# First expert's low weight parts behind its index list, its rows turned in four banks, second token tables at a later expert, last logits by halves

## The chip, the cores and the metric

The kernel runs on one core of one Trainium2 chip. The metric is the device time of one execution in microseconds (us), lower is better. Engines are named as the profile names them: PE (TensorE matmul; PEld is its weight load), DVE (VectorE), ACT (ScalarE), POOL (GpSimd), SP (SyncE, which issues plain DMAs here). Each engine works through its own list of instructions in the order in which the program wrote them.

## The reference, cut to what matters

One transformer layer over 2048 tokens of width 1024. A mixer (windowed attention and a bidirectional mLSTM) makes `x`, and then an expert layer in which each of 16 experts takes the 256 tokens with the highest affinity to it:

```
aff = softmax(h @ w_router)                    # 2048 x 16
gate, idx = top_k(aff.T, 256)                  # per expert
xg = h[idx]                                    # 16 x 256 x 1024
g, u = xg @ w_gate, xg @ w_up                  # 1024 -> 512
y = (silu(g) * u) @ w_down * gate              # 512 -> 1024
x = x + g2 * scatter_add(y at idx)
```

## The kernel before, in words

The mixer runs over 16 token tiles of 128 rows; each finished tile is normalised (`finish`), its router logits are made (`logits`, L2131) and its affinities are put into a table `aff` (`affinity`). After the last tile the expert phase (`phase_moe`) begins.

**Routing** (`route`). The 256th highest affinity of every expert is found by a search of 15 rounds (`search`, `counts`): DVE counts for two candidates (L2292), ACT for the third (L2280), PE sums (L2304, L2307), DVE takes the next candidates (L2331). Then come prefix sums, the position of every chosen token (L2441) and its split into two hexadecimal digits (`pb`, `pa`, L2448 and L2451). `picks` and `lists` turn the digits into index lists: one-hot tables on DVE, 16 matmuls over the token tiles (L2579), a small product `lm` (L2583 or L2585), one more matmul with a spreading matrix (L2590), `lw` (L2593) and `idx` (L2598). There are three lists: expert 0 alone, then experts 1 to 7, then experts 8 to 15. The tables of the two large lists take 32 DVE operations each (L2559, L2562) and lie in two of the four `y` buffers.

**Experts.** For expert e, POOL gathers its 256 rows in two tiles of 128 (`gathers`, L2610), PE turns them (16 transposes, L2628, two PSUM banks named `t`), ACT scales (`xv`, L2652), DVE casts to the high part (`xg_hi`, L2656), and DVE or POOL makes the low part (`less`, L2457). All matmuls use a high and a low part of each operand, three products each. PE makes gate and up columns in four units of 48 matmuls (`gu`, L2684), then 48 matmuls with the down weights (`yp`, L2736). `glu` and `silu_mul` make the hidden rows between them (`sg`, `h_hi`, `h_lo`). DVE scales the result into `y` (L2750), and POOL scatters it with an add into `out_x` (L2756), two scatters per expert.

**Weights.** Each expert has six pieces of 1 MB, loaded by SP (L2474) into five buffers `ew_raw`, split by ACT into `ew_hi` (L2529) and by DVE or POOL into `ew_lo` (L2457). Expert 0's first four pieces are split by quarters during routing: the high quarters (`high`, L2498) and the low quarters (`low`, L2490) are put one by one into the search rounds by `counts`, and what is left is put after it by `rest`.

**What sets the order.** A planner (`Flow`) runs the program as tasks in Python: each task says which engine it wants next and a guessed cost; a task gets an engine when it is ready and has the lowest number among those waiting (`PRE` lists these numbers; `main`, the expert matmuls, has 13). `Tokens` stand for buffers: a task that has taken one keeps it until `give`. The order in which the planner hands out the engines is the order of each engine's list on the chip; nothing is reordered there.

Of the kernel before, what the change touches and what calls it, by code (L numbers as in the profile page):

```python
# [59 lines left out]
PRE = dict(fill=2, route=3, w=3, oh=2, ol=9, gv=6, x=5, main=13, ws=1, wl=12, xs=8, h=13, down=0, y=2)  # L60
# [296 lines left out]
class Kernel:  # L357
# [1752 lines left out]
    def logits(self, i, users):  # L2110
# [16 lines left out]
        yield tok["t"]  # L2127
        pr = self.buf(self.ps, "t", [128, 16])
        yield "P", 1.73
        for k in range(8):  # L2130
            nc.tensor.matmul(pr, lhsT=xt[:, k, :], rhs=self.wr[:, k, :], start=(k == 0), stop=(k == 7))  # L2131
# [4 lines left out]
        fl.give(tok["t"])  # L2136
# [106 lines left out]
    def phase_moe(self):  # L2243
        nc, tc, a, s = self.nc, self.tc, self.a, self.s
        with ExitStack() as st:
# [15 lines left out]
            self.got, self.list_ev, self.gv_ev = Event(), evs(NE), evs(NE)  # L2261
            self.x_ev = [evs(4) for _ in range(NE)]
# [7 lines left out]
    def counts(self, x, cand, need, col, after):  # L2270
# [15 lines left out]
        lows = self.lo_todo[:1] if self.round > 4 else []  # L2286
        del self.lo_todo[:len(lows)]
# [10 lines left out]
        for g in lows:  # L2298
            self.fl.spawn(g, PRE["fill"])
# [45 lines left out]
    def route(self):  # L2345
# [90 lines left out]
        for hf in range(2):  # L2436
            nc.tensor.transpose(pt[:, hf, :], sel[:, hf * 128:(hf + 1) * 128], self.ident)
        pos = T([128, 2, 16, 8], "pos", I32)
# [65 lines left out]
    def rest(self):  # L2504
        while self.hi_todo or self.lo_todo:
            if self.hi_todo:
                yield from self.hi_todo.pop(0)
            if self.lo_todo:
                yield from self.lo_todo.pop(0)
# [22 lines left out]
    def picks(self):  # L2532

        nc, fl, keep = self.nc, self.fl, self.keep
        yield self.routed
        self.rp.__exit__(None, None, None)
        self.pg = self.pool("pgather", 2)
        p16 = self.p16
        oh = [keep.tile([128, 16, 16], F16, name=f"oh0{i}") for i in range(2)]
        for i in range(2):  # L2540
            yield V(256)
            nc.vector.tensor_tensor(oh[i], p16[i][:, 0, :, 0:1].to_broadcast([128, 16, 16]),
# [4 lines left out]
        yield from self.lists(0, 1, *oh)  # L2547
        fl.fire(self.list_ev[0])
        tok = self.tok["y"]
        for q in range(2):  # L2550
            oh = []
            if q:
                yield self.x_ev[1][3]
            for i in range(2):
                yield tok
                oh.append(self.buf(self.pin, "y", [128, D]).bitcast(F16).rearrange("p (c k e) -> p c k e", c=16, k=16))
            for k in range(16):
                yield V2(128)
                nc.vector.tensor_scalar(oh[0][:, :, k, :], p16[0][:, q], float(k), None, op0=OP.is_equal)  # L2559
                fl.follow()  # L2560
                yield V(128)
                nc.vector.scalar_tensor_tensor(oh[1][:, :, k, :], p16[1][:, q], float(k + 1),  # L2562
                                               self.ids[:, :, None].to_broadcast([128, 16, 8]), op0=OP.is_equal, op1=OP.mult)
                fl.follow()
            if q:
                yield self.x_ev[2][3]
            yield from self.lists(8 * q, 8, *(o.rearrange("p c k e -> p c (k e)") for o in oh))
            for j in range(max(8 * q, 1), 8 * q + 8):
                fl.fire(self.list_ev[j])
            for i in range(2):  # L2570
                fl.give(tok)

    def lists(self, e, n, ob, oa):
        nc, pg, fl, tok = self.nc, self.pg, self.fl, self.tok
# [11 lines left out]
        fl.give(tok["t"])  # L2586
        yield tok["t"]
# [12 lines left out]
    def gathers(self):  # L2600
        nc, s, fl, tok = self.nc, self.s, self.fl, self.tok
        for e in range(NE):
# [17 lines left out]
            self.xt[e] = hi, lo  # L2620
            for k2 in range(4):
                yield tok["t"]
                pt = self.buf(self.ps, "t", [128, 2, 256])
                yield "P", 0.43
                for j in range(2):
                    for t in range(2):
                        k = 2 * k2 + j
                        nc.tensor.transpose(pt[:, j, t * 128:(t + 1) * 128], xgs[t][:, k * 128:(k + 1) * 128], self.ident)  # L2628
                fl.spawn(self.xsplit(e, k2, pt, hi, lo), PRE["xs"])
# [15 lines left out]
    def xsplit(self, e, k2, pt, hi, lo):  # L2645
# [3 lines left out]
        for j in range(2):  # L2649
            k = 2 * k2 + j  # L2650
            yield "A", 0.45
            nc.scalar.activation(xv[:, j, :], pt[:, j, :], AF.Identity, bias=self.sh2[:, k:k + 1], scale=self.sc2[:, k:k + 1])  # L2652
        fl.give(tok["t"])
        h = hi[:, 2 * k2:2 * k2 + 2, :]
        yield V2(512)
        nc.vector.tensor_copy(h, xv)  # L2656
        yield from self.less((XSUB0 if e == 0 else XSUB)[k2], 512, lo[:, 2 * k2:2 * k2 + 2, :], xv, f(h))
# [167 lines left out]
```

## Time and profile before

| | us |
|---|---|
| median of 3 runs (lowest, highest) | 2040.84 (2037.56, 2042.3) |
| the profiled execution's own time | 2042.06 |
| span of its instructions | 2040.3 |
| PE busy, share of the span | 1863.0, 91% |
| DVE busy | 1595.5, 78% |
| ACT busy | 1280.7, 63% |
| POOL busy | 839.1, 41% |

The mixer takes the first 1400 us. The profiled execution is 1.2 us above the median of the runs. The profile's chain of what ended last gives 56% of the span to PE and 24% to DVE.

### The profile page before, as it was taken

How to read it: one execution, taken by the hardware profiler on the slowest of the kernel's cores; microseconds unless marked ns; L12 is line 12 of the kernel's file. 1: busy time of each engine (PE TensorE's matmuls, PEld its weight loads, DVE VectorE, ACT ScalarE, POOL GpSimd, SP SyncE). 2: the span in 40 equal slices, each digit the busy share in tenths (PEclk: the TensorE clock that was granted, in tenths of full speed). 3: DMA queues.
4: the chain of work that ended last, by engine and by line, in shares of the span. 5: the costliest groups of instructions: out<-in, count | busy, mean ns of one | idle time of the engine just before them, and what ended most of it. 6: DMA issues, size and time to landing. Idle time of an engine off the chain costs nothing.

```text
span 2040.3 us, 37000 instructions
## 1 busy us (share of the span) xinstructions
PE 1863.0 (91%) x12921; PEld 1665.6 (82%) x12921; DVE 1595.5 (78%) x3486; ACT 1280.7 (63%) x3144; POOL 839.1 (41%) x820
## 2 busy tenths in 40 slices
PE   7799999999999999996989989994589999999997
PEld 2698998899889989985767767783589999999996
DVE  3799779998998699868999677756667878787772
ACT  4477777787787777775665578865344545454542
POOL 0324234333543243316777665510334535353432
PEclk9899999999999999996999989996699999999999
DMA  8343264345342333227777867646467878888772
GB/s 281 98 145 102 73 189 123 109 149 160 99 120 79 95 84 97 79 82 205 270 255 260 286 224 242 225 145 222 133 203 210 261 226 253 240 235 254 223 233 42
DMA packets 293499, 357.82 MB, mean 175 GB/s; under 512 B 27288, under 2 KB 225592, under 8 KB 292416
## 3 DMA queue, kind: packets, MB, share of 16 engines
q1 hardware_dynamic: 283072, 320.32, 49.9%
q0 software_dynamic: 9376, 34.08, 7.2%
q8 instruction: 102, 1.67, 0.3%
q10 hardware_dynamic: 864, 1.05, 0.1%
q14 instruction: 85, 0.70, 0.1%
HBM read 270.73 MB, written 84.54 MB: 174 GB/s over the span
## 4 chain that ended last, share of the span: by engine, by line
PE 56%; DVE 24%; ACT 8%; DMA 6%; issue 5%; SPq 1%; POOL 0%; POOLq 0%; DVEq 0%; ACTq 0%
PE gu L2684 17%; PE mm L758 9%; PE yp L2736 8%; PE po L2004 5%; DVE w_lo L741 3%; PE t L303 2%; DMA w_raw<-in_w_in 2%; PE s L258 2%; PE o L593 1%; PE t L2628 1%; PE h L1912 1%; PE o L332 1%; PE o L331 1%; PE mm L776 1%; DVE s L280 1%
## 5 line engine op out<-in xcount | busy, mean ns | idle before, releaser
L2529 ACT ACTIVATE ew_hi<-ew_raw 128x1024 fp32r<-128x1024 f32 x184 | 193.6, 1056 | 163.6 <-PE yp L2736 91.5
L2457 DVE TENSOR_TENSOR ew_lo<-ew_raw,ew_hi 128x1024 fp32r<-128x1024 f32 x152 | 215.6, 1428 | 42.0 <-ACT ew_hi L2529 21.4
L291 POOL TENSOR_SCALAR P<-P,am 128x640 f32<-128x640 f32 (+1 forms) x128 | 113.1, 885 | 257.7 <-DVE am L289 145.4
L741 DVE TENSOR_TENSOR w_lo<-w_raw,w_hi 128x256 fp32r<-128x256 f32 (+1 forms) x352 | 157.3, 471 | 30.2 <-ACT w_hi L735 28.1
L2756 POOL DMA_INDIRECT out_x<-y,idx x32 | 57.1, 1786 | 260.7 <-DVE y L2750 175.0
L2684 PE MATMUL gu<-xg_hi,ew_hi 128*128 128x256 f32 x1024 | 148.6, 283 | 0.6 <-DVE xg_hi L2656 0.6
L758 PE MATMUL mm<-w_hi,hx_hi 128*128 128x256 f32 (+1 forms) x944 | 142.5, 288 | 5.2 <-ACT hxr L933 2.2
L735 ACT ACTIVATE w_hi<-w_raw 128x256 fp32r<-128x256 f32 (+1 forms) x352 | 135.2, 410 | 18.9 <-DMA w_raw<-in_w_in 18.1
L758 PE MATMUL mm<-w_hi,hx_lo 128*128 128x256 f32 (+1 forms) x944 | 141.9, 288 | 0.0
L2684 PE MATMUL gu<-xg_lo,ew_hi 128*128 128x256 f32 x1024 | 141.7, 280 | 0.0
L758 PE MATMUL mm<-w_lo,hx_hi 128*128 128x256 f32 (+1 forms) x944 | 141.5, 286 | 0.0
L2684 PE MATMUL gu<-xg_hi,ew_lo 128*128 128x256 f32 x1024 | 141.2, 280 | 0.0
L758 PEld LDWEIGHTS mm<-w_hi,hx_hi 128*128 128x128 f32 x944 | 124.8, 190 | 9.4 <-issue 2.7
L2684 PEld LDWEIGHTS gu<-xg_hi,ew_hi 128*128 128x128 f32 x1024 | 131.2, 189 | 1.0 <-DVE xg_hi L2656 0.9
L2684 PEld LDWEIGHTS gu<-xg_lo,ew_hi 128*128 128x128 f32 x1024 | 129.2, 189 | 0.0
L2684 PEld LDWEIGHTS gu<-xg_hi,ew_lo 128*128 128x128 f32 x1024 | 128.8, 189 | 0.0
L758 PEld LDWEIGHTS mm<-w_hi,hx_lo 128*128 128x128 f32 x944 | 125.0, 191 | 3.3 <-issue 2.6
L758 PEld LDWEIGHTS mm<-w_lo,hx_hi 128*128 128x128 f32 x944 | 124.6, 189 | 1.8 <-issue 0.9
L314 DVE TENSOR_TENSOR pl<-t,ph 128x512 fp32r<-128x512 f32 x156 | 105.8, 684 | 24.4 <-ACT ph L312 23.1
L282 ACT ACTIVATE P<-s,am 128x640 f32<-128x640 f32 (+1 forms) x128 | 99.8, 780 | 31.1 <-DVE am L280 25.7
L2750 DVE SCALAR_TENSOR_TENSOR y<-yp,gv,g2b 128x512 f32<-128x512 f32 x64 | 48.1, 751 | 90.2 <-PE yp L2736 90.2
L280 DVE CUSTOM_DVE_ANT_0 s<-s,mrow,nsink 128x640 f32<-128x640 f32 (+1 forms) x120 | 105.3, 877 | 13.1 <-PE s L262 7.5
(482 smaller groups left out, 5616.4 us busy)
## 6 DMA issues: line engine op xcount, KB each, us to landing
w_raw<-in_w_in SPq DMA_DIRECT2D x176, 256.0 KB
ew_raw<-in_w_gate SPq DMA_DIRECT2D x32, 1024.0 KB
ew_raw<-in_w_up SPq DMA_DIRECT2D x32, 1024.0 KB
ew_raw<-in_w_down SPq DMA_DIRECT2D x32, 1024.0 KB
xt<-in_w_mod SPq DMA_DIRECT2D x64, 256.0 KB
out_x<-xl SPq DMA_DIRECT2D x32, 512.0 KB
s_vs<-vsl SPq DMA_DIRECT2D x16, 516.0 KB
vsl<-s_vs SPq DMA_DIRECT2D x16, 516.0 KB
```

The costliest lines, as they stand in the source:

```text
L280: nc.vector.tensor_tensor_reduce(x, x, mask, 1.0, k.nsink[:, h:h + 1], op0=OP.add, op1=OP.min, accum_out=m[:, 0:1])
L282: nc.scalar.activation(P[:, :n], sc, AF.Exp, bias=m[:, 0:1], scale=-1.0, accum_out=m[:, 1:2])
L291: nc.gpsimd.tensor_scalar(P[:, :n], P[:, :n], m[:, 4:5], 0.0, op0=OP.mult, op1=OP.add)
L314: nc.vector.tensor_sub(lo, pt, f(hi))
L735: nc.scalar.activation(hi, raw[:, k:k + 2, :n], AF.Copy)
L741: nc.vector.tensor_sub(lo, raw[:, k:k + 2, :n], f(hi))
L758: self.nc.tensor.matmul(ps[:, :2 * n].rearrange("p (a b) -> p a b", a=2), lhsT=hx[:, k, t * 128:(t + 1) * 128], rhs=w[:, sl:sl + 2, k, :n] ...
L2004: self.nc.tensor.matmul(po, lhsT=m[:, k, :], rhs=self.wo[k0 + k][wi][:, sl], start=(j == 0), stop=(j == 11))
L2457: (self.nc.vector if eng == "D" else self.nc.gpsimd).tensor_sub(out, x, y)
L2529: nc.scalar.activation(hi[:, sl], raw[:, sl], AF.Copy)
L2684: nc.tensor.matmul(po[:, ft, :], lhsT=w[:, k, ft * 128:(ft + 1) * 128], rhs=x[:, k, :], start=(j == 0), stop=(j == 23))
L2736: nc.tensor.matmul(po[hf], lhsT=hs[i][h][:, ft, t * 128:(t + 1) * 128], rhs=wd[i][w][:, ft, hf * 512:(hf + 1) * 512], start=(j[hf] == 0), ...
```

## The change

1. `logits`: for the last two tiles the eight logit matmuls accumulate in a bank of `h2` and are issued in two halves of four, each behind its own half of the transposes.
2. The low quarters of expert 0's weights leave `counts` and `rest`; a new task `lows` issues them once expert 0's index list is made (first eight with number 1, the others with number 9).
3. `route` splits the positions of expert 0 by themselves first (16 columns in place of 256), so `picks` can begin its list before the large split.
4. `gathers`: the transposes of expert 0 go into four banks (two `t`, two `yp`), first all of the first row tile, then all of the second; one of its four scalings goes from ACT to DVE; the first product of `expert` waits for the high parts alone (`xh_ev`).
5. The tables of the two large lists become tasks `group(0)` and `group(1)` with numbers 10 and 14: group 0 waits for expert 0's rows to be split, group 1 for those of expert 3, its list for those of expert 4, and the second matmul of that list for expert 5's first piece.

```diff
-PRE = dict(fill=2, route=3, ..., main=13, ...)
+PRE = dict(fill=1, wl0=9, g0=10, g1=14, route=3, ..., main=13, ...)
...
@@ logits
+        last = i >= 2 * NT - 2
+        if last:
+            yield tok["h2"]
+            pr = self.buf(self.ps, "h2", [128, 2, 512])[:, 0, 0:16]
...
+            if last:
+                yield "P", 0.87
+                for k in range(4 * j, 4 * j + 4):
+                    nc.tensor.matmul(pr, lhsT=xt[:, k, :], rhs=self.wr[:, k, :], start=(k == 0), stop=(k == 7))
...
@@ counts
-        lows = self.lo_todo[:1] if self.round > 4 else []
-        del self.lo_todo[:len(lows)]
...
-        for g in lows:
-            self.fl.spawn(g, PRE["fill"])
...
@@ route
+        pos = T([128, 2, 8], "pos0", I32)
+        nc.vector.tensor_scalar(pos, pt[:, :, 0:8], 15.0, None, op0=OP.add)
...
+        fl.fire(self.routed0)
...
@@ rest
+    def lows(self):
+        yield self.hi_ev
+        for k in range(8):
+            yield from self.lo_todo.pop(0)
+        if self.lo_todo:
+            self.fl.spawn(self.lows(), PRE["wl0"])
...
@@ picks
+        fl.spawn(self.lows(), PRE["fill"])
         for q in range(2):
...
+            fl.spawn(self.group(q), PRE[f"g{q}"])
+
+    def group(self, q):
+        nc, fl, tok, p16 = self.nc, self.fl, self.tok["y"], self.p16
+        yield self.x_ev[3 * q][3]
...
+        if q:
+            yield self.x_ev[4][3]
+        yield from self.lists(8 * q, 8, *(o.rearrange("p c k e -> p c (k e)") for o in oh), q and self.x_ev[5][0])
...
@@ lists
+        if late:
+            yield late
         yield tok["t"]
...
@@ gathers
+            tags, pts = ("t", "t", "yp", "yp"), []
...
+            for k2 in range(4 if e == 0 else 0):
+                yield tok[tags[k2]]
+                pts.append(self.buf(self.ps, tags[k2], [128, 2, 256]))
+                yield "P", 0.22
+                turn(k2, (0,))
...
@@ expert
-                            yield self.x_ev[e][2 * k4]
-                            yield self.x_ev[e][2 * k4 + 1]
+                            for ev in (self.x_ev if xi else self.xh_ev)[e][2 * k4:2 * k4 + 2]:
+                                yield ev
```

**How the lists of the engines move.** PE, between expert 7's down product and expert 8's first columns (`yp` down product, `gu` columns, `t<-cst,xg` transposes of gathered rows, `spread` the last matmul of an index list). Before:

```order
L2736 MATMUL yp<-ew_lo,h_hi 128x512
L2628 MATMUL t<-cst,xg 128x128 x8
L2684 MATMUL gu<-xg_hi,ew_hi 128x256 x4
L2684 MATMUL gu<-xg_lo,ew_hi 128x256 x8
L2684 MATMUL gu<-xg_hi,ew_lo 128x256 x8
```

After:

```order
L2786 MATMUL yp<-ew_lo,h_hi 128x512
L2619 LDWEIGHTS spread
L2619 MATMUL t<-lm_22473,spread 128x128
L2656 MATMUL t<-cst,xg 128x128 x16
L2734 MATMUL gu<-xg_hi,ew_hi 128x256 x8
L2734 MATMUL gu<-xg_lo,ew_hi 128x256 x8
L2734 MATMUL gu<-xg_hi,ew_lo 128x256 x8
```

The last matmul of the list of experts 8 to 15 now stands behind the whole down product of expert 7, and all 16 transposes of expert 8 stand behind it, ahead of its first columns. Before, this list was made during expert 1, and the transposes here were those of expert 9.

POOL at the same place (`out_x` the scatter of an expert, `xg` a gather). Before, from expert 7's two scatters on:

```order
L2756 DMA out_x<-y,idx 2048x1024 x2
L2610 DMA xg<-s_xn,idx 128x1040
L2457 TENSOR_TENSOR xg_lo<-xv,xg_hi 128x512
L2610 DMA xg<-s_xn,idx 128x1040
L2457 TENSOR_TENSOR ew_lo<-ew_raw,ew_hi 128x1024
```

After, from expert 6's two scatters on:

```order
L2806 DMA out_x<-y,idx 2048x1024 x2
L2476 TENSOR_TENSOR ew_lo<-ew_raw,ew_hi 128x1024 x2
L2806 DMA out_x<-y,idx 2048x1024 x2
L2639 DMA xg<-s_xn,idx 128x1040 x2
L2476 TENSOR_TENSOR ew_lo<-ew_raw,ew_hi 128x1024
L2639 DMA xg<-s_xn,idx 128x1040
```

Between the scatters of expert 6 and those of expert 7 there is no gather any more; both gathers of expert 8 stand behind expert 7's second scatter.

DVE from the end of the selection to expert 0's index list, in the program after (`oh` the one-hot tables of expert 0, `pb` and `pa` the digits of all tokens):

```order
L2454 CAST p_19453<-part_19457 128x16
L2563 TENSOR_TENSOR oh_19460<-p_19452,lc 128x256
L2563 TENSOR_TENSOR oh_19461<-p_19453,lc 128x256
L2567 TENSOR_TENSOR oh_19461<-oh_19461,lc 128x256
L2460 TENSOR_SCALAR pos<-t 128x128 x2
L2467 TENSOR_SCALAR part_19469<-pos 128x256
L2470 CAST pb<-part_19469 128x256
L2467 TENSOR_SCALAR part_19489<-pos 128x256
L2470 CAST pa<-part_19489 128x256
L2610 CAST lm_19486<-t 16x16
L2622 TENSOR_TENSOR lw_19495<-t,lc 128x16
L2627 TENSOR_REDUCE idx<-lw_19495 128x2
```

Before, the six wide operations on `pos`, `part`, `pb` and `pa` stood ahead of the tables `oh`, and `lm` stood directly behind them; now they stand between `oh` and `lm`. Behind `idx` 11 low quarters follow in a row, where the 32 table operations of the first large list stood.

## Rows read from the trace of the kernel before

**Rows 1.** Busy us and instructions per engine in three stretches; PEclk is the granted clock.
```profile
core 0: us, PE busy (x) PEld busy (x) DVE busy (x) ACT busy (x) POOL busy (x), PEclk, DMA share, GB/s
1400.04:1458.88 58.84, 12.60 (x105) 9.73 (x106) 45.48 (x214) 21.41 (x54) 6.77 (x7) 0.50 0.61 203
1458.88:1543.98 85.10, 79.37 (x569) 74.30 (x570) 54.58 (x89) 38.53 (x53) 30.51 (x19) 0.96 0.59 175
1543.98:1579.04 35.06, 35.06 (x258) 33.12 (x258) 26.73 (x25) 17.93 (x25) 16.17 (x10) 1.00 0.82 241
```

**Rows 2.** Timeline, two rounds without a low quarter: start us, us, engine, instruction.
```profile
1405.13 0.16 DVE L2331 SCALAR_TENSOR_TENSOR cand<-hits,base 128x3 f32<-128x3 f32 x1
...
1406.78 0.16 DVE L2331 SCALAR_TENSOR_TENSOR cand<-hits,base 128x3 f32<-128x3 f32 x1
```

**Rows 3.** Chain of work that ended last, routing and expert 3: start us, us, what.
```profile
1417.46 0.17 DVE cand L2331
...
1428.70 0.17 DVE cand L2331
...
1431.65 0.45 issue
...
1437.08 0.60 DVE ew_lo L2490
...
1438.86 0.50 DVE pos L2441 x2
...
1442.93 0.18 DVE idx L2598
...
1579.04 19.61 PE gu L2684 x168
```

**Rows 4.** Timeline, end of the mixer and start of expert 0.
```profile
1394.46 1.96 PE L2131 MATMUL t<-wr,hx2t 128*128 128x16 f32 x16 [0.50 <-DVE lg L2135]
...
1445.62 1.12 POOL L2610 DMA_INDIRECT xg<-s_xn,idx  x1 [0.30 <-issue]
...
1447.73 0.28 DVE L2562 SCALAR_TENSOR_TENSOR y<-pa,lc 128x128 f16<-128x128 f16 x1
...
1451.34 0.15 DVE L2641 COPY gv<-xg 128x1 f32<-128x1 f32 x1 [1.03 <-DMA xg<-s_xn,idx]
...
1452.76 1.97 PE L2628 MATMUL t<-cst,xg 128*128 128x128 f32 x8 [0.38 <-DVE lw L2593]
...
1458.88 0.80 PE L2684 MATMUL gu<-xg_hi,ew_hi 128*128 128x256 f32 x2 [0.65 <-DVE xg_hi L2656]
```

**Rows 5.** Timeline, experts 0 and 1, where the second large list is made.
```profile
1475.69 6.71 DVE L2559 TENSOR_SCALAR y<-pb 128x128 f16<-128x128 f16 x1
...
1477.56 4.77 POOL L2457 TENSOR_TENSOR ew_lo<-ew_raw,ew_hi 128x1024 fp32r<-128x1024 f32 x2
...
1492.34 0.56 PE L2736 MATMUL yp<-ew_hi,h_hi 128*128 128x512 f32 x1
...
1514.68 0.23 PE L2590 MATMUL t<-lm,spread 128*128 128x128 f16 x1 [2.85 <-DVE lm L2585]
```

**Rows 6.** Timeline, the boundary between two experts in the steady stretch.
```profile
1574.33 1.03 PE L2628 MATMUL t<-cst,xg 128*128 128x128 f32 x8
...
1577.11 2.06 POOL L2756 DMA_INDIRECT out_x<-y,idx  x1 [5.39 <-DVE ew_lo L2457]
1579.47 1.01 POOL L2610 DMA_INDIRECT xg<-s_xn,idx  x1 [0.30 <-issue]
...
1580.28 3.76 DVE L2457 TENSOR_TENSOR ew_lo<-ew_raw,ew_hi 128x1024 fp32r<-128x1024 f32 x2 [1.28 <-issue]
...
1581.98 1.78 POOL L2610 DMA_INDIRECT xg<-s_xn,idx  x1 [0.17 <-issue]
...
1598.21 0.69 DVE L2707 TENSOR_TENSOR sg<-sg,gu 128x512 f32<-128x512 f32 x1 [0.89 <-PE gu L2684]
```

**Rows 7.** The gather's line, all 32: time from issue to landing.
```profile
DMA to landing us min/median/max: 4.1/7.7/9.5
```

More of the change, by code (lines that the diff above doesn't have):

```diff
@@ L2125, in logits @@
             fl.give(tok["t"])
+            if last:
+                yield "P", 0.87
+                for k in range(4 * j, 4 * j + 4):
+                    nc.tensor.matmul(pr, lhsT=xt[:, k, :], rhs=self.wr[:, k, :], start=(k == 0), stop=(k == 7))
         self.release(users)
[L2127 to L2131, printed above, removed]
+        if not last:
+            yield tok["t"]
+            pr = self.buf(self.ps, "t", [128, 16])
+            yield "P", 1.73
+            for k in range(8):
+                nc.tensor.matmul(pr, lhsT=xt[:, k, :], rhs=self.wr[:, k, :], start=(k == 0), stop=(k == 7))
         fl.give(tok["hx2t"])
@@ L2437, in route @@
             nc.tensor.transpose(pt[:, hf, :], sel[:, hf * 128:(hf + 1) * 128], self.ident)
+        pos = T([128, 2, 8], "pos0", I32)
+        yield V(16)
+        nc.vector.tensor_scalar(pos, pt[:, :, 0:8], 15.0, None, op0=OP.add)
+        fl.follow()
+        self.p0 = [T([128, 16], f"p0{i}", F16) for i in range(2)]
+        for i, (op, n) in enumerate(((OP.bitwise_and, 15), (OP.logical_shift_right, 4))):
+            part = T([128, 16], f"part0{i}", I32)
+            yield V(16)
+            nc.vector.tensor_scalar(part, pos.rearrange("p h g -> p (h g)"), n, None, op0=op)
+            fl.follow()
+            yield V(16)
+            nc.vector.tensor_copy(self.p0[i], part)
+            fl.follow()
+        fl.fire(self.routed0)
         pos = T([128, 2, 16, 8], "pos", I32)
@@ L2504, in rest @@
     def rest(self):
[L2505 to L2509, printed above, removed]
+        while self.hi_todo:
+            yield from self.hi_todo.pop(0)
+        self.fl.fire(self.hi_ev)
+    def lows(self):
+        yield self.hi_ev
+        for k in range(8):
+            yield from self.lo_todo.pop(0)
+        if self.lo_todo:
+            self.fl.spawn(self.lows(), PRE["wl0"])
     def wsplit(self, e, j, raw, shape):
@@ L2547, in picks @@
         yield from self.lists(0, 1, *oh)
+        yield self.routed
+        self.rp.__exit__(None, None, None)
+        self.pg = self.pool("pgather", 2)
         fl.fire(self.list_ev[0])
-        tok = self.tok["y"]
+        fl.spawn(self.lows(), PRE["fill"])
         for q in range(2):
[L2551 to L2571, printed above, removed]
@@ L2573, in lists @@
-    def lists(self, e, n, ob, oa):
-        nc, pg, fl, tok = self.nc, self.pg, self.fl, self.tok
+            fl.spawn(self.group(q), PRE[f"g{q}"])
+    def group(self, q):
+        nc, fl, tok, p16 = self.nc, self.fl, self.tok["y"], self.p16
+        yield self.x_ev[3 * q][3]
+        oh = []
+        for i in range(2):
+            yield tok
+            oh.append(self.buf(self.pin, "y", [128, D]).bitcast(F16).rearrange("p (c k e) -> p c k e", c=16, k=16))
+        for k in range(16):
+            yield V2(128)
+            nc.vector.tensor_scalar(oh[0][:, :, k, :], p16[0][:, q], float(k), None, op0=OP.is_equal)
+            fl.follow()
+            yield V(128)
+            nc.vector.scalar_tensor_tensor(oh[1][:, :, k, :], p16[1][:, q], float(k + 1),
+                                           self.ids[:, :, None].to_broadcast([128, 16, 8]), op0=OP.is_equal, op1=OP.mult)
+            fl.follow()
+        if q:
+            yield self.x_ev[4][3]
+        yield from self.lists(8 * q, 8, *(o.rearrange("p c k e -> p c (k e)") for o in oh), q and self.x_ev[5][0])
+        for j in range(max(8 * q, 1), 8 * q + 8):
+            fl.fire(self.list_ev[j])
+        for i in range(2):
+            fl.give(tok)
@@ L2575, in lists @@
+    def lists(self, e, n, ob, oa, late=None):
+        nc, pg, fl, tok = self.nc, self.keep, self.fl, self.tok
         yield tok["t"]
@@ L2650, in xsplit @@
             k = 2 * k2 + j
-            yield "A", 0.45
-            nc.scalar.activation(xv[:, j, :], pt[:, j, :], AF.Identity, bias=self.sh2[:, k:k + 1], scale=self.sc2[:, k:k + 1])
-        fl.give(tok["t"])
+            sh, sc = self.sh2[:, k:k + 1], self.sc2[:, k:k + 1]
+            if e == 0 and k2 == 1:
+                yield V(256)
+                nc.vector.tensor_scalar(xv[:, j, :], pt[:, j, :], sc, sh, op0=OP.mult, op1=OP.add)
+                fl.follow()
+            else:
+                yield "A", 0.45
+                nc.scalar.activation(xv[:, j, :], pt[:, j, :], AF.Identity, bias=sh, scale=sc)
+        fl.give(tok[tag])
         h = hi[:, 2 * k2:2 * k2 + 2, :]
```

40 lines of the change are left out of this document (22 added, 18 removed).

## The prediction

> **What bounds the kernel now.** I read the busy time by stretches first, to see which engine sets the pace where. Two stretches matter [rows 1]. From 1400 to 1458.88 us the kernel routes: PE works 12.6 of 58.8 us at a granted clock of 0.50 (the level of 1.2 GHz), DVE 45.5, and everything waits for one thread of search, prefix sums, index list, gather and turning. From 1543.98 on PE is busy for all of an expert's 35.06 us at clock 1.00 (2.4 GHz), so PE alone sets the pace there: what delays PE is added to the end, and what other engines gain or lose behind its back costs nothing. Between them, from 1458.88 to 1543.98, PE is already on expert work but has gaps. Then I read the chain of work that ended last for routing [rows 3] and the timelines for the gather and the gaps [rows 4 to 6].
>
> How large are the gaps? A steady expert is 192 gu, 48 yp and 16 transposes in 35.06 us [rows 1], a gu 19.61/168 = 0.117 us [rows 3]. The program has 402 gu, 96 yp, 48 transposes and 16 table products in the 85.1 us. That is two experts (70.1), 18 more gu (2.1), 16 more transposes (1.7) and some 1.1 for the table products: 75.0 us. So 10.1 us are lost. The clock averages 0.96, which is 3.4 us lost to two stretches at the lower level, 1.7 each: one at the start, one after the wait that ended at 1492.34 [rows 5]. The other 6.7 us are waits. Both have the second large list as their cause: a table operation of DVE was held for 6.71 us while POOL made low parts for 4.77 us, what stood behind it on DVE (expert 1's hidden rows) came late, and later PE stood 2.85 us before the list's spreading matmul for DVE's `lm` [rows 5]. That last row also shows that PE does not step over an instruction that waits, although columns of the same expert stood ready behind it.
>
> **The change part by part**, against the profiled execution's own 2042.06 us (gains negative):
>
> *Last logits by halves: 0.* Half of the last 16 passes, 1.96/2 = 1.0 us [rows 4], can leave the end of the thread. But in the new order ACT makes the second half's copy behind the scaling and the exponential of the tile before, so as much can be lost. Bounds -1.0 and +1.0; I take the middle.
>
> *Low quarters out of the rounds: -2.3.* A round with one takes (1428.70 - 1417.46)/6 = 1.87 us [rows 3], one without 1.65 [rows 2]. Eleven had one; the first of these waits for ACT and the first weight load anyway, so 10 x 0.22. Bounds -2.5 and -1.5.
>
> *Five low quarters behind the search: -2.6.* Each stood alone on the chain, 0.60 [rows 3], the first of them half hidden; 4 x 0.55 + 0.4. Bounds -3.0 and -2.0.
>
> *Positions of expert 0 first: +0.3.* Before, 1438.86 to 1443.1 [rows 3]. The small split takes five short operations, but the wide ones (1.6 us) now stand between `oh` and `lm`, where DVE waited only 0.7 us for PE: 0.9 shorter ahead of the tables, 0.9 longer behind, and 0.3 for waits between five dependent operations. Bounds -0.5 and +0.8.
>
> *Gather of expert 0: +2.0.* Its second tile landed at 1451.34, 5.7 us after the issue at 1445.62 [rows 4]. Beside it DVE now makes 11 low quarters, and each piece of weights so finished frees a buffer and lets SP load another 1 MB, two of them in this window. In the steady stretch, with both beside it, landing takes 7.7 us at the median [rows 7]: +2.0. Bounds 0 and +4.5 (9.5 at most, and the issue lengthened as next). The issue alone took 1.78 us beside DVE's low parts where another took 1.01 [rows 6]. The Trainium skill, page "SBUF — State Buffer", section "Who interferes with whom", says that a tensor_tensor between two SBUF tiles, as a low part is, should not hold up POOL's descriptor work, unlike a tensor_scalar in a two-port mode, as the tables were; by that the gather would be freed rather than hindered on DVE's side and this term would be about 1.2. The trace does not bear it out: the issue of 1.78 us ran beside low parts.
>
> *Four banks: -2.3.* Before, from 1451.34 to free-running gu at 1458.88, 7.5 us with 6 gu done [rows 4]. After, eight transposes are left when the second tile lands, 2.0 us at 1.97/8 each; ACT's and DVE's scalings and DVE's four casts overlap, and the last cast ends some 5 us after landing, with 4 gu done: -2.5 + 0.2. Bounds -3.5 and -0.5.
>
> *The stretch that follows: -6.7.* Of the 10.1 us lost, one cold clock (1.7) stays. The first large list is now made during expert 0: its tables follow DVE's casts and are done before PE has made 72 gu, `lm` costs PE 0.2. Expert 1's rows are gathered about 20 us into expert 0, when PE reaches their transposes: 1.0, and 0.5 for the banks. 10.1 - 3.4. Bounds -8.4 and -3.7.
>
> *Second tables beside expert 2: +3.5.* They go to DVE once expert 3's rows are split, in expert 2's time. The 32 operations took 5.0 us (1443.0 to 1448.0) [rows 3, 4]; 30 stand before the second `sg` of expert 2, where such an `sg` waited 0.9 us for PE, DVE's time to spare [rows 6]. So it is 3.8 late; the down product gives 0.7 back; 0.4 for POOL's single low parts. Bounds 0, and 10.9 (rival 2).
>
> *Second list behind expert 7: +22.0.* This decides. `group(1)` has number 14, expert matmuls 13, so the planner gives its 16 products to PE only when no column is left, and the list is finished behind expert 7's down product. Until then POOL cannot gather for expert 8, and PE has only expert 8's transposes next. I read the wait from the same boundary [rows 6], with E = 1574.33 as the end of the down product. POOL's second scatter runs at E + 2.8 (it waits for the first), the first gather at E + 5.1, the second straight behind it at E + 6.5; `idx` needs only E + 1.7. Landing +7.7 [rows 7]: E + 14.2. From there to free-running gu as for expert 0 before, 7.5: E + 21.7. Less 6 gu (0.7) and 16 transposes that expert 7 no longer carries (1.7), plus one cold clock (1.7) and 1.0 for this list's 16 products (in the stretch above the first large list's have taken their place): 22.0. Bounds: 4.1 for landing and 6.8 for turning, 17; 9.5, 24. The experts behind cannot make it up: PE is busy all the time.
>
> **Sum:** -2.3 - 2.6 + 0.3 + 2.0 - 2.3 - 6.7 + 3.5 + 22.0 = +13.9, or 2056.0 for an execution like the profiled one. That one lies 1.2 above the median, so **2054.7 us**.
>
> **The rivals.**
> 1. *The wait is paid back (not slower).* While PE stands before expert 8, DVE, ACT and the loads run ahead as far as the buffers go. If experts 9 to 15 are in truth held by these, each could run 3 us shorter, and 22.0 becomes nothing: -8.1, 2032.7 us. It decides only if an expert takes under 34.5 us after the wait; PE's 35.06 of 35.06 speaks against it.
> 2. *The second tables collide with POOL as before.* If a table operation is held for the 6.7 us again [rows 5], `sg` is 3.8 + 6.1 late, PE stands 9.2 and restarts cold, 10.9 in place of 3.5: 2062.1 us. For it: POOL makes low parts during expert 2 too. Against: one at a time, not two in a row.
> 3. *The first gather starves.* +4.5 in place of 2.0, and expert 1's gather, late by the same loads, lets PE wait 3 us more: 2060.2 us.
> 4. *Less lost and more won*, all at the near bounds (gather 0, banks -3.5, stretch -8.4, tables 0, list 17): -2.3 - 2.6 + 0.3 - 3.5 - 8.4 + 17 = +0.5, 2041.3 us, no change.
>
> **How the numbers follow.** Forecast 0.60 (its own range 2047 to 2059, from the gather's and list's bounds); rival 1 0.06, rival 2 0.12, rival 3 0.12, rival 4 0.10. The predicted time is the forecast's, 2054.7. A range of 2044 to 2063 holds the forecast and rivals 2 and 3 and leaves out 1 and 4, 0.16. A difference under 0.2% (4.1 us) cannot be told from no change: faster 0.06 (rival 1), same 0.10 (rival 4), slower 0.84.
>
> **What would show it.** Right: the list's `idx` for expert 0 some 4.5 us earlier after the search's start; rounds of 1.65 us throughout; expert 3's long run of gu starting some 8 us earlier than at 1579.04 [rows 3]; and between expert 7's down product and expert 8's gu a gap of PE of about 20 us that ends on a gather, with the clock at 0.5 in it. Wrong: PE without a gap there, or one under 12 us, or DVE's tables costing PE more than that gap.

## The result, and the profile after

The changed kernel takes 2061.53 us (median of 4 runs, 2056.1 to 2063.64), the kernel before 2041.57 us (4 runs, 2037.56 to 2043.16). The ratio is 1.0097 with a 95% interval of 1.0072 to 1.0121: slower by 20 us, inside the predicted range and 6.8 us above the predicted time. The profiled execution took 2061.25 us, its span 2059.5.

Busy time by stretches of the changed kernel, cut at the same events as [rows 1]: routing, from there to expert 2's long run of gu, the gap behind expert 7, and an expert of the steady stretch.

```profile
core 0: us, PE busy (x) PEld busy (x) DVE busy (x) ACT busy (x) POOL busy (x), PEclk, DMA share, GB/s
1403.12:1458.75 55.63, 12.83 (x97) 9.83 (x97) 43.80 (x186) 20.26 (x52) 5.95 (x5) 0.50 0.56 183
1458.75:1536.57 77.82, 77.17 (x560) 72.44 (x561) 58.65 (x89) 38.32 (x53) 34.11 (x20) 0.98 0.69 210
...
1744.77:1769.37 24.60, 7.05 (x32) 5.43 (x31) 7.41 (x14) 5.93 (x10) 12.66 (x9) 0.65 0.67 201
...
1829.03:1864.22 35.19, 35.19 (x257) 33.23 (x257) 26.73 (x26) 17.93 (x24) 16.08 (x9) 1.00 0.80 238
```

Routing is 3.2 us shorter than in [rows 1], and PE loses 0.65 us to waits in the stretch behind it instead of 5.7 (span less busy time of the second row, here and in [rows 1]). An expert near the end is as long as before (35.19, PE busy throughout). New is the third row: 24.6 us in which PE is busy for 7.05.

Four pieces of the chain of work that ended last: two rounds of the search, the index list, expert 3's gu.

```profile
1419.35 0.17 DVE cand L2336
...
1420.99 0.17 DVE cand L2336
...
1440.60 0.18 DVE idx L2627
...
1575.92 19.79 PE gu L2734 x168
```

The rounds take 1.65 us, as forecast, apart from two that are longer in both kernels (the fifth waits for the first weight load). The search starts at 1403.33 (before 1400.25) and the list ends 37.3 us behind it (before 42.7): 5.4 earlier, forecast 4.6. Expert 3's run of gu starts only 3.1 us earlier than at 1579.04 [rows 3], where 8 had been forecast.

The boundary from expert 7 to expert 8, in the timeline of the changed kernel:

```profile
1744.61 0.23 PE L2619 MATMUL t<-lm,spread 128*128 128x128 f16 x1
...
1745.79 0.38 DVE L2627 TENSOR_REDUCE idx<-lw 128x16 int32<-128x128 f32 x1
...
1747.65 2.21 POOL L2806 DMA_INDIRECT out_x<-y,idx  x1 [5.69 <-DVE ew_lo L2476]
...
1750.16 1.00 POOL L2639 DMA_INDIRECT xg<-s_xn,idx  x1 [0.31 <-issue]
...
1751.47 0.97 POOL L2639 DMA_INDIRECT xg<-s_xn,idx  x1 [0.30 <-issue]
...
1758.57 0.47 PE L2656 MATMUL t<-cst,xg 128*128 128x128 f32 x1 [13.74 <-DMA xg<-s_xn,idx]
...
1760.14 1.76 PE L2656 MATMUL t<-cst,xg 128*128 128x128 f32 x7 [1.09 <-DMA xg<-s_xn,idx]
...
1769.37 0.72 PE L2734 MATMUL gu<-xg_lo,ew_hi 128*128 128x256 f32 x2 [0.72 <-POOL xg_lo L2476]
```

This is the wait that decided the forecast. The spreading product of the second list stands behind the down product (E = 1744.6), `idx` is ready at E + 1.6, but POOL has expert 7's second scatter ahead of the gathers, which start at E + 5.6 and E + 6.9. PE waits 13.74 us for the first tile and once more for the second, which lands at E + 15.5. Free-running gu (gu that follow one another without a wait) starts at E + 24.8; E + 21.7 had been forecast, from E + 14.2 for the landing.

The second tables, on DVE in expert 2's time:

```profile
1547.39 0.91 DVE L2586 TENSOR_SCALAR y<-pb 128x128 f16<-128x128 f16 x1
...
1549.42 2.83 DVE L2476 TENSOR_TENSOR h_lo<-sg,h_hi 128x512 fp32r<-128x512 f32 x1
...
1560.35 0.50 PE L2786 MATMUL yp<-ew_hi,h_hi 128*128 128x512 f32 x1 [1.84 <-ACT h_hi L2762]
...
1561.72 0.80 PE L2786 MATMUL yp<-ew_hi,h_lo 128*128 128x512 f32 x1 [0.88 <-DVE h_lo L2476]
```

30 of the 32 operations, three low parts and an `h_lo` that was held for 2.83 us stand ahead of the second `sg`. PE waits 1.84 and 0.88 us in the down product and runs on at the lower level of the clock (granted 0.55 from 1561.7 to 1565, 1.00 behind it).

### The profile page after: what moved, and what is told of

It reads as the page before. It is cut to its first block, busy times and chain, and to the rows that moved or that the text cites. A ratio compares the mean times of both kernels' runs of the same rounds, so it can differ in the third digit from the quotient of the medians.

```text
span 2059.5 us, 37003 instructions
## 1 busy us (share of the span) xinstructions
PE 1868.8 (91%) x12921; PEld 1667.1 (81%) x12921; DVE 1591.9 (77%) x3493; ACT 1278.7 (62%) x3142; POOL 841.6 (41%) x820
## 4 chain that ended last, share of the span: by engine, by line
PE 54%; DVE 23%; ACT 9%; DMA 7%; issue 5%; POOL 2%; SPq 1%; POOLq 0%; DVEq 0%; ACTq 0%
PE gu L2734 16%; PE mm L758 9%; PE yp L2786 8%; PE po L2004 4%; DVE w_lo L741 3%; PE t L303 2%; DMA w_raw<-in_w_in 2%; PE s L258 2%; PE o L593 1%; PE o L332 1%; PE t L2656 1%; PE o L331 1%; DVE s L280 1%; PE h L1912 1%; ACT w_hi L735 1%
## 5 line engine op out<-in xcount | busy, mean ns | idle before, releaser
L282 ACT ACTIVATE P<-s,am 128x640 f32<-128x640 f32 (+1 forms) x128 | 99.7, 779 | 31.8 <-DVE am L280 26.5
```

Of the source, the lines that this page charges most:

```text
L282: nc.scalar.activation(P[:, :n], sc, AF.Exp, bias=m[:, 0:1], scale=-1.0, accum_out=m[:, 1:2])
```

## The experiments

Most kernels differ by less than the runs of one kernel scatter (4 to 13 us), so I compare executions by stretches between events that every kernel has. **A**: from the start of the mixer's last `mixl` (L1972) to the first `cand` of the search. **B**: from there to expert 0's `idx`. **C**: from the first gather's issue to the first use of the second tile. **D**: from that issue to the first yp of expert 1. **E**: from there to the first yp of expert 3. **F**: from the first yp of expert 6 to that of expert 8. **G**: from the start of the search to the end of the span. All in us, from each kernel's profiled execution; the medians and ratios are those of all its runs, each ratio to runs of before on the same chip. One execution stands behind each stretch. Between executions of the same code A agrees within 0.1, F too where there is no gap in it (within 1.1 with the gap), D only within 2.5.

| kernel | median | ratio to before (95%) | A | B | C | D | E | F | G |
|---|---|---|---|---|---|---|---|---|---|
| before | 2041.57 | | 26.5 | 42.7 | 7.3 | 84.3 | 70.1 | 70.2 | 640.0 |
| changed | 2061.53 | 1.0097 (1.0072 to 1.0121) | 28.4 | 37.3 | 8.8 | 79.4 | 74.4 | 93.9 | 656.1 |
| e1 early list | 2035.08 | 0.9970 (0.9958 to 0.9982) | 28.4 | 37.6 | 8.8 | 77.9 | 73.6 | 69.7 | 630.6 |
| e2 old logits | 2058.26 | 1.0084 (1.0067 to 1.0101) | 26.5 | 37.9 | 9.7 | 79.6 | 73.0 | 94.0 | 656.1 |
| e3 old banks | 2060.84 | 1.0098 (1.0082 to 1.0114) | 28.4 | 37.3 | 8.7 | 79.4 | 74.6 | 92.8 | 655.9 |
| e4 tables over four | 2039.12 | 0.9983 (0.9972 to 0.9994) | 28.4 | 37.3 | 9.6 | 80.4 | 69.7 | 69.7 | 636.9 |
| e5 e1 + old logits | 2033.81 | 0.9952 (0.9937 to 0.9967) | 26.5 | 37.9 | 8.8 | 78.2 | 73.6 | 69.7 | 631.4 |
| e6 e5 + tables over three | 2031.83 | 0.9941 (0.9928 to 0.9954) | 26.5 | 37.9 | 8.7 | 78.4 | 70.0 | 69.7 | 629.8 |
| e7 e5 + loads held | 2035.48 | 0.9959 (0.9943 to 0.9975) | 26.5 | 37.8 | 7.0 | 76.4 | 73.6 | 69.7 | 629.3 |
| e8 e5 + quarters late | 2052.86 (one) | | 26.5 | 37.9 | 6.6 | 96.7 | 73.6 | 69.7 | 650.2 |
| e9 e6 + loads held | 2030.56 | 0.9947 (0.9930 to 0.9965) | 26.5 | 37.9 | 7.1 | 77.1 | 70.0 | 69.7 | 628.7 |
| e10 e9 + quarters first | 2029.24 | 0.9935 (0.9917 to 0.9954) | 26.5 | 37.8 | 7.4 | 76.7 | 70.1 | 69.7 | 628.2 |
| e11 e10 + old banks | 2030.29 | 0.9938 (0.9919 to 0.9957) | 26.5 | 38.6 | 6.8 | 77.1 | 70.0 | 69.7 | 628.9 |

**e1: the second list in time.** What follows the tables in `group` becomes a task `large` of its own.

```diff
+        fl.spawn(self.large(q, oh), PRE["gl"])     # gl=10
+
+    def large(self, q, oh):
+        fl, tok = self.fl, self.tok["y"]
         yield from self.lists(8 * q, 8, ..., q and self.x_ev[5][0])
```

> The changed kernel, but the list of experts 8 to 15 (its 16 products, lm, the spreading product, lw and idx) runs as a task of its own with number 10, ahead of the expert matmuls' 13; its tables keep number 14 and their place. My theory: the gap behind expert 7's down product comes from number 14 alone, and nothing of it is paid back later. The two experts around it took 23.7 us more than two steady ones, so the time falls by 22 to 24, to about 2038.5 us, and PE has no wait between experts 7 and 8. Rival A (the wait was partly paid back, because other engines ran ahead during it): a fall of 8 to 16 only, 2045 to 2053 us, with experts 9 to 15 longer than the 35.0 us that they take now. Rival B (the list is held by its wait for expert 5's first piece or by its late tables): nothing changes, 2061 us.

Measured: 2035.08 us, a fall of 26.5. F is 69.7 and not 93.9, which is 24.2 of it; D and E are another 1.5 and 0.8 shorter, although their code is the same but for the place of the 16 products, mainly because the granted clock rose earlier in e1's first expert and did not fall in expert 2, as told in the section on the prediction. The chain at the same boundary, PE without a gap:

```profile
1732.36 10.93 PE yp L2790 x48
1743.28 0.88 PE t L2660 x8
1744.16 2.73 PE gu L2738 x24
```

Number 14 is the cause: moving the list alone takes the gap away. And nothing of the gap had been paid back: from the first yp of expert 8 to the end it is 266.3 us here, 265.9 in the changed kernel, 266.4 before. Rivals A and B fall. This kernel is the first that beats the kernel before.

**e2: the last logits as before.**

```diff
-        last = i >= 2 * NT - 2
+        last = False
```

> The changed kernel with the last logits made as before, in one pass of eight. In the changed kernel the search begins 3.1 us later than before. My theory now: some 1.9 of it are the new order of PE and ACT at the end of the mixer (the second half of the last tile's logits stands behind a transpose that waits for DVE), the rest is the mixer, which ran 1.2 late already before these logits. So the search begins 1.9 to 3.1 us earlier, near 1400.3 to 1401.5 us, and the time falls to 2058.5 to 2059.6 us. Rival (all of the 3.1 is how this execution's mixer ran): the search begins within 0.5 us of 1403.3 and the time stays at 2061.5.

A is 26.5 in every kernel with the old logits and 28.4 in every one with the new: 1.9 us, so the rival falls. The rest of the 3.1 is when the mixer ends, and that lies within what executions differ by: the last `mixl` started at 1370.8 to 1379.8 us in the profiled executions of the 13 kernels. Where the 1.9 goes stands in the timeline of the changed kernel:

```profile
1395.50 0.66 PE L2126 MATMUL t<-cst,xl 128*128 128x128 f32 x4
...
1396.53 1.13 ACT L2160 ACTIVATE xn<-xl,xrs 128x1024 f32<-128x1024 f32 x1
...
1397.86 0.57 ACT L2128 ACTIVATE hx2t<-t 128x512 f32<-128x512 f32 x1
...
1398.73 1.73 PE L2133 MATMUL h<-wr,hx2t 128*128 128x16 f32 x8
...
1400.50 0.17 DVE L2144 COPY lg<-h 128x16 f32<-128x16 f32 x1 [0.98 <-PE h L2133]
```

The transposes of the second half are done at 1396.2, but ACT has `xn` and the exponential of the tile before ahead of the copy, which ends at 1398.4; only then can the second half of the logits run. The transpose that I had blamed runs at 1398.57, between the two, and cost 0.3 at most. The time fell by 3.3. Of the 1.9, 0.6 is lost again in B, since the search still waits for the first weight load (its fifth round takes 4.05 us in place of 3.44), so 1.3 is left and the other 2.0 are scatter.

**e3: two banks for expert 0.** `gathers` and `xsplit` as before for all experts.

> The changed kernel with expert 0's 16 transposes in two banks as before, all four scalings on ACT; the first products still wait for high parts alone. From the landing of the second tile to free-running gu the changed kernel takes 8.3 us with 16 gu done before, the kernel before 7.5 with 6. The prediction's step: four banks are worth 2.3, so without them the stretch from the landing to the down product of expert 1 is 2.3 us longer and the time 2063.8. My theory now: what ends last is the low parts of the rows, which stand behind low quarters of the weights on DVE, so banks are worth 0.5: 2062. Rival: the banks cost something (two yp banks, one scaling taken from ACT): 1 us shorter, 2060.5.

D is 79.4 in both. With four banks expert 0's first yp stood 34.2 us behind the landing, with two 35.1, but from there to expert 1's the two-bank kernel took 35.7 and the four-bank kernel 36.4. So 0.9 is won, and 0.8 lost in expert 1. That loss is not shown to be the banks': eight gu of expert 1 took 0.907 us in the two-bank kernel and 0.942 in the four-bank one, which is 0.84 us over 192 gu, and the cause of this pace was not found (last section). The prediction's 2.3 did not come. The gather and the turning in the timeline of the changed kernel:

```profile
1441.69 1.24 POOL L2639 DMA_INDIRECT xg<-s_xn,idx  x1 [35.59 <-DVE idx L2627]
...
1443.24 1.39 POOL L2639 DMA_INDIRECT xg<-s_xn,idx  x1 [0.30 <-issue]
...
1443.24 0.37 SPq L2493 DMA_DIRECT2D ew_raw<-in_w_down  x1
...
1445.65 0.37 SPq L2493 DMA_DIRECT2D ew_raw<-in_w_gate  x1
...
1450.49 0.15 DVE L2684 COPY gv<-xg 128x1 f32<-128x1 f32 x1 [2.44 <-DMA xg<-s_xn,idx]
...
1454.11 1.22 PE L2734 MATMUL gu<-xg_hi,ew_hi 128*128 128x256 f32 x4 [1.63 <-DVE xg_hi L2705]
...
1454.58 1.83 DVE L2705 CAST xg_hi<-xv 128x512 fp32r<-128x512 f32 x2
...
1456.13 1.22 PE L2734 MATMUL gu<-xg_hi,ew_hi 128*128 128x256 f32 x4 [0.79 <-DVE xg_hi L2705]
```

The casts end at 1456.4, 5.9 us behind the landing (forecast "some 5"); two of them took 1.83 us beside a low part on POOL. PE waits 1.63 and 0.79 us for casts, the second time until 5.6 us behind the landing, with 4 gu done. Then a low quarter took 1.76 us on DVE (alone 0.6) ahead of the last low part of the rows, but PE had other gu to do and stood only 0.12 us for it at 1458.75. With two banks (e3) the last wait for a cast ended 6.5 us behind the landing, also with 4 gu done. SP's loads beside the gather are e7's matter.

**e4: the tables over four experts** (early list kept; the list's own two waits, for expert 4's rows and for expert 5's first piece, are left out).

```diff
         for k in range(16):
+            if q and k in {4: 4, 8: 5, 12: 6}:
+                yield self.x_ev[{4: 4, 8: 5, 12: 6}[k]][3]
```

> As the run with the early list, and the 32 table operations of that list are dealt out, eight in each of the times of experts 2 to 5, in place of all 32 in expert 2's. In the changed kernel they made expert 2's down product wait 1.84 and 0.88 us and PE lost another 1.7 at the low clock: 4.3 in all. My theory: eight operations are 1.3 us, DVE has 0.9 to spare ahead of the second sg and the down product 0.7, so nothing waits, and the time is 4.3 below the run with the early list, about 2034 us. Rival A (DVE has nothing to spare in truth, each expert pays its part): equal to the early list's run, 2038.5. Rival B (two y buffers held over four experts more hold up the results of the down products): PE waits at yp and the time is above 2038.5.

The time is 2039.12, above e1. Expert 2's loss is gone (E 69.7), but a new one stands in expert 5 (its yp 42.1 us behind expert 4's):

```profile
1663.93 0.28 DVE L2591 SCALAR_TENSOR_TENSOR y<-pa,lc 128x128 f16<-128x128 f16 x1
...
1664.26 1.89 PE L2610 MATMUL t<-y 128*128 128x128 f16 x16 [4.00 <-DVE y L2591]
```

The planner had put the 16 products where it thought the last table done; on the chip DVE was late, and PE, which takes nothing out of order, stood 4.0 us and restarted at the lower level of the clock (granted 0.50 from 1664.26 to 1668; the products took 1.89 us, 1.07 in the changed kernel). e4 moved the products as well as the tables, so it does not say what dealing out alone is worth; e6 does. None of the three theories had it; neither rival is supported, since PE lost nothing in experts 2 to 4.

**e5: early list and old logits.**

> The run with the early list, and the last logits made as before. In the runs so far, from the mixer's last low part (L1972) to the start of the search it took 26.5 us with the old logits and 28.4 with the new ones, so the time falls by 1.9 from the early list's 2035.1, to 2033.2 us. Rival: the mixer's end is hidden behind the first weight load (the search waits for it in its fifth round), so nothing is gained: 2035.1.

Measured 1.3 below e1, A 1.9 shorter and B 0.4 longer: part of the gain is behind the first weight load, as the rival says (the fifth round takes 4.08 us, 3.71 in e1), but not all. The difference of the medians is within their scatter.

**e6: tables over experts 1 to 3**, list behind expert 5's rows, its spreading product one expert later.

```diff
+            if q and k % 6 == 0:
+                yield self.x_ev[2 + k // 6][3]
...
-            yield self.x_ev[4][3]
+            yield self.x_ev[5][3]
```

> The run before this one (early list, old logits), and the tables of the second list dealt out over experts 1 to 3 (12, 12 and 8 operations), its products placed in expert 4's second half and its spreading product in expert 5, so that PE meets neither before DVE is done. In the run that dealt them out over experts 2 to 5, expert 2's loss of 4.3 us was gone, but PE waited 4.00 us for the last table and ran cold after it. My theory: with room behind the last table both losses are gone, 3.9 to 4.4 below the run before this one: about 2029 us. Rival (12 operations are 1.9 us, more than the 0.9 that DVE has to spare ahead of the second sg, and PE waits in experts 1 and 2 in place of one wait): 1 us below, 2032.

The windows of e6 from expert 2's first yp to expert 3's and from there to expert 4's (columns as in the first block; the 16 products are in the second):

```profile
1550.01:1585.52 35.51, 35.51 (x258) 33.24 (x257) 28.73 (x35) 17.96 (x24) 16.43 (x9) 1.00 0.82 242
1585.52:1621.34 35.82, 35.82 (x274) 33.81 (x273) 26.92 (x27) 17.93 (x24) 16.05 (x9) 1.00 0.81 238
```

PE is busy for the whole of both, and for the 34.47 us ahead of them, so no wait is left and the rival falls. But G fell by 1.6 and the median by 2.0, not by 3.9. I had taken the changed kernel's 4.3, but in e5 the tables cost only the two waits, 1.85 and 0.87 us: the clock stayed at 1.00 there, and 0.9 of E are the 16 products, which lie behind E in e6. Of these 2.7 another 0.8 is lost to PE's pace in the experts that follow, which have no waits in either kernel (see the last section).

**e7 and e8: what slows the first gather.** e7 holds the weight loads by a small transfer behind the gathers; e8 holds the low quarters, and with them the loads, since `lows` begins with a wait for `gv_ev[0]`. In e7 the buffers that low quarters free are given back only behind this transfer, so that SP's loads stand behind it:

```diff
+                nc.sync.dma_start(s["mo"][0:128, 0:4], xgs[1][:, 0:4])
```

> Early list, old logits, and SP's weight loads from the second down piece on stand behind a small transfer of 2 KB out of expert 0's second gathered tile, so none of them starts before that tile has landed; DVE's low quarters stay where they are. From the first gather's issue to the second tile's use it took 7.3 us in the kernel before, and 8.7 to 9.7 in all runs with the change. If the weight loads on the DMA engines are the cause: 7.3 or less. If it is DVE's low quarters (which slow POOL's descriptors): 8.7 to 9.7 as it was. The time as a whole may rise, since expert 0's and 1's weights come 5 us later; the landing decides.

> Early list, old logits, and all 16 low quarters of expert 0 stand on DVE behind the landing of its rows (the weight loads that they release are then late too). DVE does nothing during the gather. Both causes are away: the first issue to the second tile's use falls to 7.3 us or less by either theory; if it stays at 9, neither low quarters nor loads are the cause. What follows is 5 to 8 us longer, because the 16 quarters (9.6 us) then stand among the casts of the rows.

The timeline of e7, where SP's first load (1451.28) stands behind the landing:

```profile
1443.79 1.24 POOL L2648 DMA_INDIRECT xg<-s_xn,idx  x1 [35.62 <-DVE idx L2636]
...
1450.76 0.34 SPq L2653 DMA_DIRECT2D s_mo<-xg  x1
...
1450.77 0.15 DVE L2695 COPY gv<-xg 128x1 f32<-128x1 f32 x1 [0.63 <-DMA xg<-s_xn,idx]
...
1451.28 0.37 SPq L2494 DMA_DIRECT2D ew_raw<-in_w_down  x1
```

C is 7.0 in e7, though 11 low quarters run beside the gather as before, and 6.6 in e8. So the loads are the cause of most of it: 8.8 in e5, 7.0 without them. In the 4 us behind the second gather's issue the 16 DMA engines are busy for 1.02 of the time in e5 and 0.70 in e7. The window of e5 (columns as in the first block):

```profile
1447.60:1451.60 4.00, 1.97 (x8) 1.57 (x8) 3.42 (x7) 0.00 (x0) 0.00 (x0) 0.50 1.02 404
```

The same of e7:

```profile
1446.70:1450.70 4.00, 1.97 (x8) 1.57 (x8) 3.44 (x7) 0.00 (x0) 0.01 (x1) 0.50 0.70 225
```

The Trainium skill, page "DMA: Bandwidth & Descriptors", section "Issuing engines are not separate DMA queues", says that transfers from all issuing engines run on the same 16 DMA engines and interleave; e5 and e7 agree, since SP's loads delay POOL's gather. The low quarters cost some of the rest, as e8's issues without them show:

```profile
1439.88 1.09 POOL L2644 DMA_INDIRECT xg<-s_xn,idx  x1 [35.76 <-DVE idx L2632]
...
1441.27 0.97 POOL L2644 DMA_INDIRECT xg<-s_xn,idx  x1 [0.30 <-issue]
...
1446.46 0.15 DVE L2689 COPY gv<-xg 128x1 f32<-128x1 f32 x1 [2.09 <-DMA xg<-s_xn,idx]
```

1.09 and 0.97 us, against 1.24 and 1.39 beside the quarters: 0.57 in all. By the rule that I weighed in the prediction (the Trainium skill, page "SBUF — State Buffer", section "Who interferes with whom") this should be nothing, and the tables of the kernel before should be what hinders; there the two issues took 1.29 and 1.12 us, in sum less than beside the quarters. The page calls its reason inferred, and the measurement decides.

What follows in e8 is not 5 to 8 us longer, as expected, but 18.5 (D 96.7 against 78.2): PE waits again in experts 0 and 1 (up to 4.0 us for a cast) and runs at a granted clock of 0.50 for two more stretches. And the medians do not show the gain of e7: its 2035.48 is 1.7 above e5's, inside the scatter; G is 2.1 shorter.

**e9 to e11: what expert 0 does with it.** e9 joins e6 and e7; e10 lets all 16 quarters follow `idx` in one go; e11 is e10 with two banks.

> Early list, old logits, tables over experts 1 to 3, and the weight loads held until expert 0's second tile has landed. Each alone shortened the time from the start of the search to the end of the span: 631.5 us with neither, 629.7 with the tables dealt out, 629.3 with the loads held. My theory: the two are independent, 627.5 us from the start of the search, and about 2030 us in all. Rival (the held loads make expert 0's and 1's weights late, which the wait in expert 2 had covered): no better than 629.7.

> As the run before this one, and all 16 low quarters of expert 0 stand directly behind the list's idx, ahead of the casts; in the kernels so far 11 stood there and five among the casts and low parts of expert 0's rows. 16 x 0.6 = 9.7 us from idx; the second tile lands 8.1 behind idx and the first cast can start 1.7 later, so the quarters end just in time. My theory: what held up PE after the turning was not banks but these five quarters, so free-running gu starts 1.5 to 2.4 us earlier after the landing, and the down product of expert 1 at least 1 us earlier. Rival (expert 0 is bound by its later weights or by DVE's other work, and gives all of it back): the down product of expert 1 starts as far behind the first gather's issue as in the run before this one (76.4 us with loads held), and the time is the same.

> As the run before this one, with expert 0's rows turned in two banks and all scalings on ACT. It tells whether four banks are worth the 2.3 us of the prediction once DVE is not the one that ends last. If DVE's order was what hid them: free-running gu starts some 2 us later after the landing than with four banks. If banks matter little in any order: within 0.8 us.

e9: the held loads won 2.1 in G in e7 (against e5); here, against e6, 1.1, between the theory and the rival. e10: D and G are 0.4 shorter, which one execution each cannot tell from nothing. PE's last wait for a cast ended hardly earlier (5.5 us behind the landing in e10, 5.7 in e9), so the theory that the five quarters were what held PE falls: with them away the low parts of the rows on DVE took 1.65 in place of 0.68 us, beside POOL's. The timeline of e10, first transposes of the second tile and second set of gu:

```profile
1446.91 1.11 PE L2668 MATMUL t<-cst,xg 128*128 128x128 f32 x4 [0.82 <-DMA xg<-s_xn,idx]
...
1452.38 1.22 PE L2746 MATMUL gu<-xg_hi,ew_hi 128*128 128x256 f32 x4 [1.13 <-DVE xg_hi L2717]
```

The same two places in e11:

```profile
1452.60 1.75 PE L2668 MATMUL t<-cst,xg 128*128 128x128 f32 x7 [1.96 <-DMA xg<-s_xn,idx]
...
1459.02 1.25 PE L2742 MATMUL gu<-xg_hi,ew_hi 128*128 128x256 f32 x4 [0.72 <-DVE xg_hi L2713]
```

5.5 us from the landing to the second set of gu with four banks, 6.4 with two: the wait ends 0.9 earlier. From the landing to expert 1's yp it is 69.3 us in e10 and 70.3 in e11, but executions of the same four-bank code differ there from 69.1 to 70.9, so what the banks are worth in time is not told. e6, e9, e10 and e11 cannot be told apart by their intervals; all are below before by 0.5 to 0.7% (0.35% at the least by the intervals), and e10 has the lowest median, 2029.24.

## Why the prediction was right

The sum was +13.9 against the profiled execution; the two spans differ by 19.2. Term by term:

| term | forecast | measured |
|---|---|---|
| where the mixer ends (last `mixl`) | none | +1.2 |
| last logits (A) | 0 (-1.0 to +1.0) | +1.9 |
| search and list (B) | -2.3 - 2.6 + 0.3 = -4.6 | -5.4 |
| gather of expert 0 (`idx` to landing) | +2.0 | +1.5 |
| four banks (landing to expert 0's 33rd gu) | -2.3 | 0.0 |
| the stretch behind (to expert 1's yp) | -6.7 | -6.4 |
| second tables (expert 1's to expert 3's yp) | +3.5 | +4.3 |
| experts 3 to 6 | 0 | -1.1 |
| second list (F) | +22.0 | +23.7 |
| expert 8 to the end | 0 | -0.5 |
| sum | +13.9 | +19.2 |

**The deciding term was right, in cause and size.** That number 14, behind the matmuls' 13, puts the list behind expert 7's down product, and that nothing makes up for it, is shown by e1. The size came out 1.7 larger, mostly because the second tile landed 8.7 us behind its issue, not 7.7, and turning took 9.2 and not 7.5, with 8 more gu done in it.

**Four banks: the step that failed.** The step forecast that PE would run free some 5 us behind the landing with 4 gu done, in place of 7.5 with 6, and counted 2.3 us for it. The wait did move like that: it ended 5.6 us behind the landing with 4 gu done. Two banks in the changed kernel give 6.5 (e3), so some 0.9 of this is the banks. The other 1.1 is most likely the first large list, whose `lw` held the transposes before [rows 4]; no run shows that alone. But the time was not won. The forecast let "one cold clock (1.7)" stay as it was; what the gu behind the last wait ran at is this, before (first row) and after (columns as in [rows 1]):

```profile
1458.88:1461.90 3.02, 3.02 (x14) 3.02 (x15) 0.67 (x1) 0.00 (x0) 0.78 (x1) 0.51 0.53 138
...
1456.13:1462.30 6.17, 6.05 (x26) 5.75 (x27) 6.17 (x25) 0.00 (x0) 1.39 (x1) 0.50 0.25 78
1462.30:1463.40 1.10, 1.10 (x12) 1.10 (x11) 1.10 (x9) 0.00 (x0) 0.00 (x0) 1.00 1.09 387
```

The granted clock rose 10.6 us behind the landing before and 11.9 after, so PE ran 6.2 us of gu at half the clock in place of 3.0, which costs the 1.6 us that the shorter wait had won. Expert 0's 33rd gu starts 12.1 us behind the landing in both. In other executions of the same code the clock rose 9.0 (e1) to 11.9 us (e4) behind the landing and the 33rd gu started at 10.8 to 12.1: up to 1.3 us of the term comes or not by that, and why the clock rose when it did is open.

**The stretch behind** was forecast nearly right, -6.7 against -6.4, and for the reason given: the waits of 2.88 and 2.85 us and the second stretch at the lower clock are gone. One reading in it was wrong: the 6.7 us of waits were what was left over of the 10.1, while [rows 1] give 85.10 - 79.37 = 5.7. Two smaller slips of the working, 10 x 0.22 as 2.3 and 17 for a lower bound that adds up to 17.7, change nothing.

**Last logits.** The step named the loss (ACT copies "behind the scaling and the exponential of the tile before") and then took the middle, 0, with a bound of 1.0. It is 1.9, outside that bound: the copy waits for all of `xn`, 1.1 us, and for `sq` ahead of it. A loss whose mechanism the order shows should not have been averaged with a gain that the same order excludes.

**Search and list.** -5.4 for -4.6; its three parts were not run apart. **Gather.** +1.5 within 0 to 4.5, and for the reasons given: loads released early (three in the window, not two), which e7 shows, and longer issues beside the low quarters (e8).

**Second tables.** +4.3 for 3.5: the waits of 1.84 and 0.88 were forecast as 3.8 less 0.7; the low clock behind them, the other 1.6, was left out. It is not in every execution: e2, the same code there, lost 2.9 with the clock at 1.00.

**Signs that failed.** Expert 3's gu came 3.1 us earlier, not 8: the mixer's end (1.2), the logits (1.9) and the banks (2.3) make up the difference. The granted clock in the gap was 0.65 on average, not 0.5: it was 0.50 only from 1749.0 to 1766.1. Of the rivals, 1 falls with e1; 2 (tables held as before) did not happen, the table operation that met POOL's low part took 0.91, not 6.7; 3 is seen in part (the landing up to 9.7 in other executions) at less than its price; 4 was far off.

## What to carry to other kernels

In a schedule that a planner writes, look at what a rank behind the main work's means on an engine that is always busy: "not until the main work runs dry", and the wait then comes at the place where the result is needed. Moving work into the shadow of a transfer frees buffers earlier, and the loads that follow collide with that same transfer. And place a product that needs another engine's late result well behind the planner's estimate: on an engine that works in order, a wait of 1 us there delays everything behind it. Last, a wait that is shortened at the lower clock need not be time won: look whether the clock rises any earlier.

## What the runs showed that I had not expected

As far as one execution of each kernel tells, the scatter lies mostly ahead of the expert phase: the mixer's last `mixl` started anywhere from 1370.8 to 1379.8 us, while in kernels with the same code A agrees within 0.1 us and F without the gap within 0.1 (D, with the gather and the rise of the clock in it, within 2.5). Cutting at an event behind the mixer told differences of 1 us that medians could not, except in D.

Eight gu took 0.933 us in every steady expert of the kernel before, but 0.907 or 0.942 in the changed ones, mostly one value within an expert, though some have both (in e1, experts 8, 11 and 14 had 34.5 us, those between 35.2 or 35.3). The granted clock was 1.00 in all of them. What sets this pace was not found; it made e6's gain 0.8 us smaller than its removed waits.
